# Storing the third group's norm factors in place of its scaled rows, and loading the mixer output's input straight into its low parts

## The chip, the cores and the metric

The kernel runs on one core of a Trainium2 chip. The metric is device time in microseconds for one execution of the whole program, the median of three runs; smaller is better. The core has a matrix engine (PE, with weight loads, PEld, beside it), VectorE (DVE), ScalarE (ACT), GpSimd (POOL) and a queue that issues the transfers (SP).

## What is computed

One inference step of a two-layer decoder, for a prompt of 1024 tokens with 16 learned tokens ahead of it and eight single-token sequences, 1048 columns in all, model width 1024. Layer 0 mixes tokens with a Conformer convolution, layer 1 with an RWKV-7 recurrence; each is followed by a squared-ReLU MLP. The parts that the change touches, from the reference:

```python
def _rmsnorm(x, g):
    xf = x.astype(jnp.float32)
    y = xf * lax.rsqrt(jnp.mean(xf * xf, axis=-1, keepdims=True) + RMS_EPS)
    return (y * g.astype(jnp.float32)).astype(x.dtype)
...
    xx = prev - h
    xr = h + xx * x_mix[0]
...
    out = ((yn + bonus).astype(h.dtype) * g) @ w_o
...
        hn = _rmsnorm(h, norm_mix[i])
...
        h = h + out
        h = h + _sqrelu_mlp(_rmsnorm(h, norm_mlp[i]), w_mlp_in[i], w_mlp_out[i])
```

In layer 1 the first argument of the mixer is the scaled row `_rmsnorm(h, norm_mix[1])`, and the residual that its output is added to is the unscaled `h`.

## The kernel before

Activations lie as 128 partitions (features) by 8 blocks (k) by tokens. Each matrix product is made of three matmuls of float32 rounded to a shorter type: every operand x is split into a high part (a cast on ACT, L159 and L177) and a low part (x minus the high part, L160 for activations and L182 for weights, on DVE or, in four pieces of 256 columns, on POOL), and `mm3` (L209 to L213) adds high·high, high·low and low·high.

The work comes in token groups. Layer 0 has three (columns 0 to 351, 352 to 699, 700 to 1047), the RWKV mixer four (0, 272, 528 and 784 onwards, 272, 256, 256 and 264 wide), mixer output and second MLP three (16, 344, 696 onwards, 328, 352, 352 wide). The mixer groups don't end where layer 0's do: mixer group 2 (528 to 783) begins in layer 0's second group and ends in its third.

At the end of layer 0 `norm_out` (L636 to L654) stores a group's MLP output to DRAM twice: unscaled to d_h (L640) and, after sums of squares on ACT, a mean on PE and a reciprocal on DVE (rs_d, L295), scaled in place by eight DVE instructions (L651, one per k) to d_hn (L654). For the third group this runs beside mixer group 0. `prepare` (L854 to L893) then loads a mixer group's scaled rows from d_hn as one tile hx (L863, L865), forms xx, the difference to the token before (L869), and later the mixes (mx, L892). For groups 1 to 3 it runs beside the v products of the group before.

Beside the mixer groups runs the recurrence over chunks of 64 tokens: loads of a chunk's factors (L1273 to L1284), a triangular inversion for every eight chunks (ni loaded at L1241, 30 pairs of DVE instructions tt and ni at L1246 and L1247, then stored to d_p at L1250 and loaded by chunk as p at L1280 and transposed to x on DVE at L1302), and per chunk a sequence of small matmuls (S, Y, gg, bT, W, po, U). `norm_gate` (L1507 to L1541) turns 128 tokens of its output into the mixer output's input and stores that to d_z.

`mixer_out` (L1629 to L1647) then, for each of the three output groups, loads h1 from d_h (L1633), loads d_z in eight pieces into temporary tiles zr of which there are three (L1639), splits each into z_h and z_l, and makes eight output columns (ps_oo) from the weights wo_0 to wo_7, adding each into h1 (L1643). The last chunks and the second MLP's first weights run beside the first of these groups. The pools used here are opened over memory that the mixer's input pools (hx, mixes and others) gave back, so that a tile can wait for the last user of the memory beneath it.

In each engine's queue instructions stand in the order that a scheduler gives them from the program's order, so a small edit can move others.

Of the kernel before, what the change touches and what calls it, by code (L numbers as in the profile page):

```python
# [16 lines left out]
P = 128  # L17
# [31 lines left out]
def hybrid_step(tc, x_prompt, x_sample, state_conv, state_shift, state_wkv, meta_tokens,  # L49
# [10 lines left out]
    with ctx:  # L60
# [12 lines left out]
        dram = pool(ctx, "dram", 1, space=bass.MemoryType.DRAM)  # L73
        d_x2 = dram.tile([P, KT, G0[2][1]], F32, name="d_x2")
        d_h = dram.tile([P, KT, T], F32, name="d_h")
        d_hn = dram.tile([P, KT, T], F32, name="d_hn")
        d_rk = dram.tile([P, KT, 2, T], F32, name="d_rk")
        d_ab = dram.tile([NCH, P, KT, 2, 2 * HS], F32, name="d_ab")
        d_v = dram.tile([NCH * HS, D], F32, name="d_v")
# [68 lines left out]
        def raw_pool(stack, tag, n, **kw):  # L148
            return pool(stack, f"wraw{tag}", 1, **kw), n

        def split_pool(stack, tag, n, **kw):
            return pool(stack, f"wsp{tag}", 1, **kw), n
# [74 lines left out]
        def dense(w, act, n, name, fill=None):  # L227
            it = dense_steps(w, act, n, name)
            while True:
# [4 lines left out]
                if fill:  # L234
                    fill()

        def new_act(pl, name, nmax, tag="act"):
            return (pl.tile([P, KT, nmax], F32R, name=f"{name}_h", tag=f"{tag}h"),
                    pl.tile([P, KT, nmax], F32R, name=f"{name}_l", tag=f"{tag}l"))

# [173 lines left out]
        with ExitStack() as le:  # L414
# [221 lines left out]
            def norm_out(g):  # L636

                c0, n = G0[g]
                hv = h[g][:, :, :n]
                nc.sync.dma_start(d_h[:, :, c0:c0 + n], hv)  # L640
                if g < 2:
                    add, parts = square_sums(n, f"d{g}", lambda k: u[g][:, k, :n], (nc.gpsimd,), "accd")
                else:
                    add, parts = square_sums(n, f"d{g}", lambda k: tt(f"sqd{k}", "t1")[:, :n], (nc.gpsimd, nc.vector))
                for k in range(KT):
                    add(k, hv[:, k, :])
                    yield MW / KT
                rs = rstd_of(mean_bcast(parts, n, f"d{g}"), n, 0, f"d{g}", "rs" if g < 2 else "rsm")
                yield 1
                for k in range(KT):  # L650
                    nc.vector.scalar_tensor_tensor(hv[:, k, :], hv[:, k, :], vec("norm_mix", KT + k), rs[:, :n],  # L651
                                                   op0=ALU.mult, op1=ALU.mult)
                    yield 1
                nc.sync.dma_start(d_hn[:, :, c0:c0 + n], hv)  # L654
# [199 lines left out]
        def prepare(g):  # L854

            c0, n = G1[g]
            npr = min(c0 + n, NP_TOK) - c0
            nm = lambda s, *a: f"{s}{g}" + "".join(f"_{x}" for x in a)

            hx = hnp.tile([P, KT, 1 + N1], F32, name=nm("hx"), tag="hx")  # L860
            if g == 0:
                nc.gpsimd.memset(hx[:, :, 0:1], 0.0)
                nc.sync.dma_start(hx[:, :, 1:1 + n], d_hn[:, :, :n])  # L863
            else:
                nc.sync.dma_start(hx[:, :, :1 + n], d_hn[:, :, c0 - 1:c0 + n])  # L865
            yield
            xx = hnp.tile([P, KT, N1], F32, name=nm("xx"), tag="xx")
            for k in range(KT):
                (nc.gpsimd if k % 3 == 2 else nc.vector).tensor_sub(xx[:, k, :npr], hx[:, k, 0:npr], hx[:, k, 1:1 + npr])  # L869
                yield  # L870
            if npr < n:
                sst = cur["raw"].tile([P, D], F32, name="sst", tag="raw")
                nc.scalar.dma_start(sst[:DEC, :], state_shift[0])
                pv = bank("pv", "x")
                for k in range(KT):
                    nc.tensor.transpose(pv[:, k * DEC:(k + 1) * DEC], sst[:DEC, k * P:(k + 1) * P], ident[:DEC, :DEC])
                sps = hnp.tile([P, KT, DEC], F32, name=nm("sps"), tag="sps")
                nc.scalar.copy(sps.rearrange("p k b -> p (k b)"), pv[:, :KT * DEC])
                nc.vector.tensor_sub(xx[:, :, npr:n], sps, hx[:, :, 1 + npr:1 + n])
                so = cur["raw"].tile([P, D], F32, name="so", tag="raw")  # L880
                for half in range(2):
                    pv = bank(f"pso{half}", "x")
                    for q in range(4):
                        nc.tensor.transpose(pv[:DEC + 1, q * P:(q + 1) * P], hx[:, half * 4 + q, npr:npr + DEC + 1], ident)
                    nc.scalar.copy(so[:DEC + 1, half * 512:(half + 1) * 512], pv[:DEC + 1, :])
                nc.scalar.dma_start(o_shift_prompt[0], so[0:1, :])
                nc.scalar.dma_start(o_shift_sample[0], so[1:DEC + 1, :])

            def mix(i, k):

                t = (cur["mx"] or cur["tmp"]).tile([P, cur["wm"]], F32, name=nm("mx", i, k), tag="t2")
                nc.vector.scalar_tensor_tensor(t[:, :n], xx[:, k, :n], vec("x_mix", i * KT + k), hx[:, k, 1:1 + n],  # L892
                                               op0=ALU.mult, op1=ALU.add)  # L893
                hi, lo = (r.tile([P, cur["wm"]], F32R, name=nm("m" + q, i, k), tag="m" + q) for q, r in zip("hl", cur["mix"]))
                split(hi[:, :n], lo[:, :n], t[:, :n], nc.gpsimd if k % 3 else nc.vector)
                return hi[:, :n], lo[:, :n]

            prep[g] = mix, hx, sps if npr < n else None
# [714 lines left out]


        with ExitStack() as l1:
            raw_f, wsp_f = raw_pool(l1, "f", 3), split_pool(l1, "f", 1)
            open_tmp(l1, N2, "2", 3)
            residp = pool(l1, "resid1", 1)
            actp = pool(l1, "actp1", 1)
            hidp = pool(l1, "hidp1", 2)  # L1620
            lf = l1.enter_context(ExitStack())
            wsp_g = split_pool(lf, "g", 1)
            cur.update(rings((raw_a, raw_f), (wsp_a, wsp_f, wsp_g)))
# [5 lines left out]
            def mixer_out(g, residp, actp, fill, add, order=range(KT), early=None):  # L1629
                ready = None  # L1630
                lo, n = G2[g]
                h1 = hl[g] = residp.tile([P, KT, cur["wide"]], F32, name=f"h1_{g}", tag="h")
                nc.sync.dma_start(h1[:, :, :n], d_h[:, :, lo:lo + n])  # L1633
                if early:
                    ready = early(h1)
                z = new_act(actp, f"z{g}", cur["wide"])
                for p in range(KT):
                    t = tt(f"zr{g}{p}", "t1")
                    nc.sync.dma_start(t[:, :n], d_z[:, p, lo:lo + n])  # L1639
                    split(z[0][:, p, :n], z[1][:, p, :n], t[:, :n], nc.vector)  # L1640
                for i, m in enumerate(order):
                    ps = dense(load_col(rwkv_w_o[0], m, f"wo{g}_{m}", nc.vector if early else nc.gpsimd), z, n, f"oo{g}_{m}", fill)
                    nc.vector.tensor_add(h1[:, m, :n], h1[:, m, :n], ps[:, :n])  # L1643
                    add(i, h1[:, m, :n])
                    if ready:
                        ready(m)
                    fill()  # L1647
# [326 lines left out]
```

## Time and profile before

| | |
|---|---|
| median of 3 runs | 2756.64 us (2746.97 to 2761.95) |
| the profiled execution | 2760.69 us |
| its span in the trace | 2758.7 us |
| granted PE clock, mean over the span | 0.971 |
| PE busy | 2585.6 us (94%) |
| PEld busy | 2495.6 us (90%) |
| DVE busy | 2074.5 us (75%) |
| POOL busy | 1710.2 us (62%) |
| ACT busy | 1404.5 us (51%) |
| mean DRAM traffic | 155 GB/s |

All times in the trace are microseconds from the span's start. PE, busy 94% of the span, is the engine whose gaps the profile is read for: a gap names the engine that released it, and a low granted clock behind a gap makes the matmuls there longer. A row of a timeline is one instruction or several equal ones, with its start, its time, engine, line, operation, result and operands; what stands in brackets is the idle time ahead of it and who ended that.

### The profile page before, as it was taken

Reading aid. Unit: us, or ns where it says so; the run is one execution under the profiler, and the core shown is the slowest. Engines: PE = TensorE matmul, PEld = TensorE weight load, DVE = VectorE, ACT = ScalarE, POOL = GpSimd, SP = SyncE. Lnnn points to the kernel's source line nnn. Section 1 sums busy time; section 2 is a strip of 40 time slices with the busy share of each in tenths; the row PEclk is TensorE's granted clock in tenths of the full one; section 3 lists DMA queues with packets and bytes.
Section 4 is the critical chain, followed back from the end, with each engine's and each line's share of the span. In section 5 each row is a group of like instructions: output and inputs, shape, how many; then the busy total and the mean of one; then the engine's idle time right before and its main releaser. Section 6 shows DMA issues by size and latency. Waiting matters only on the chain.

```text
span 2758.7 us, 54194 instructions
## 1 busy us (share of the span) xinstructions
PE 2585.6 (94%) x20362; PEld 2495.6 (90%) x20362; DVE 2074.5 (75%) x3868; ACT 1404.5 (51%) x2614; POOL 1710.2 (62%) x2259
## 2 busy tenths in 40 slices
PE   8998999999998999997898798979989999999998
PEld 7998999899997999996788687768989998999998
DVE  5999999997456554677988887677897687566565
ACT  5545444553355444565675775655544564333333
POOL 6686877887787444554553544547648856556663
PEclk9998999999999999999999999989999999999999
DMA  6563544445445446668796886887657642222221
GB/s 181 159 192 92 161 132 137 134 148 164 138 131 150 146 142 179 185 199 220 204 241 187 219 221 175 198 230 186 178 140 232 175 131 78 76 70 77 69 77 58
DMA packets 659283, 428.30 MB, mean 155 GB/s; under 512 B 126840, under 2 KB 609208, under 8 KB 659022
## 3 DMA queue, kind: packets, MB, share of 16 engines
q1 hardware_dynamic: 652780, 421.93, 55.0%
q10 hardware_dynamic: 6018, 2.89, 0.4%
q8 instruction: 160, 2.62, 0.4%
q14 instruction: 101, 0.83, 0.1%
q0 software_dynamic: 224, 0.03, 0.0%
HBM read 353.03 MB, written 72.66 MB: 154 GB/s over the span
## 4 chain that ended last, share of the span: by engine, by line
PE 64%; DVE 15%; DMA 7%; POOL 5%; ACT 4%; issue 4%; SPq 0%; POOLq 0%; ACTq 0%; DVEq 0%
PE ps_in L212 4%; PE ps_in L213 4%; PE ps_in L211 4%; PE out L212 4%; PE out L213 4%; PE out L211 4%; PE os L213 3%; PE os L211 3%; PE os L212 3%; POOL wo_lo L182 2%; POOL wi_lo L182 2%; DVE cv L552 2%; PE su L211 1%; PE su L213 1%; PE su L212 1%
## 5 line engine op out<-in xcount | busy, mean ns | idle before, releaser
L182 POOL TENSOR_TENSOR wo_lo<-wo_raw,wo_hi 128x256 fp32r<-128x256 f32 x512 | 398.1, 810 | 188.1 <-ACT wo_hi L177 149.0
L182 POOL TENSOR_TENSOR wi_lo<-wi_raw,wi_hi 128x256 fp32r<-128x256 f32 x472 | 373.3, 824 | 161.0 <-ACT wi_hi L177 150.3
L552 DVE SCALAR_TENSOR_TENSOR cv<-u,wdw,cv 128x352 f32<-128x352 f32 (+2 forms) x720 | 376.4, 572 | 0.7
L211 PE MATMUL out<-hh,wo_hi 128*128 128x348 f32 (+2 forms) x1024 | 332.2, 328 | 17.8 <-DVE h L382 6.9
L212 PE MATMUL out<-hh,wo_lo 128*128 128x348 f32 (+2 forms) x1024 | 330.8, 324 | 2.6 <-DVE wo_lo L182 2.6
L211 PE MATMUL ps_in<-m_h,wi_hi 128*128 128x348 f32 (+2 forms) x1024 | 329.7, 322 | 2.2 <-ACT wi_hi L177 1.4
L212 PE MATMUL ps_in<-m_h,wi_lo 128*128 128x348 f32 (+2 forms) x1024 | 328.6, 321 | 2.4 <-POOL wi_lo L182 2.4
L213 PE MATMUL ps_in<-m_l,wi_hi 128*128 128x348 f32 (+2 forms) x1024 | 327.8, 321 | 0.0
L213 PE MATMUL out<-hl,wo_hi 128*128 128x348 f32 (+2 forms) x1024 | 327.1, 323 | 0.0
L382 DVE TENSOR_TENSOR h<-h,out 128x348 f32<-128x348 f32 (+2 forms) x512 | 249.8, 503 | 68.8 <-PE out L213 68.1
L177 ACT CAST wo_hi<-wo_raw 128x1024 fp32r<-128x1024 f32 x152 | 159.3, 1049 | 203.0 <-PE ps_in L213 104.9
L177 ACT CAST wi_hi<-wi_raw 128x1024 fp32r<-128x1024 f32 x128 | 134.2, 1049 | 235.0 <-PE out L213 105.2
L211 PEld LDWEIGHTS out<-hh,wo_hi 128*128 128x128 f32 x1024 | 194.0, 190 | 24.7 <-DVE h L382 8.2
L212 PEld LDWEIGHTS out<-hh,wo_lo 128*128 128x128 f32 x1024 | 195.1, 191 | 4.5 <-DVE wo_lo L182 3.2
L211 PEld LDWEIGHTS ps_in<-m_h,wi_hi 128*128 128x128 f32 x1024 | 192.8, 188 | 4.6 <-ACT wi_hi L177 2.6
L212 PEld LDWEIGHTS ps_in<-m_h,wi_lo 128*128 128x128 f32 x1024 | 192.6, 188 | 3.8 <-POOL wi_lo L182 2.8
L213 PEld LDWEIGHTS out<-hl,wo_hi 128*128 128x128 f32 x1024 | 193.5, 190 | 1.0 <-DVE hl L160 0.5
L213 PEld LDWEIGHTS ps_in<-m_l,wi_hi 128*128 128x128 f32 x1024 | 192.3, 188 | 0.8 <-DVE m_l L305 0.2
L1859 DVE TENSOR_TENSOR h<-h,os 128x352 f32<-128x352 f32 x256 | 126.5, 515 | 58.7 <-PE os L213 58.2
L212 PE MATMUL os<-hhs,wos_lo 128*128 128x352 f32 x512 | 165.1, 323 | 0.0
L213 PE MATMUL os<-hls,wos_hi 128*128 128x352 f32 x512 | 164.1, 323 | 0.0
L211 PE MATMUL os<-hhs,wos_hi 128*128 128x352 f32 x512 | 155.3, 323 | 0.1
(501 smaller groups left out, 8040.3 us busy)
## 6 DMA issues: line engine op xcount, KB each, us to landing
wi_raw<-in_w_mlp_in_dram SPq DMA_DIRECT2D x128, 512.0 KB
wo_raw<-in_w_mlp_out_dram SPq DMA_DIRECT2D x128, 512.0 KB
wk_raw<-in_rwkv_w_k_dram SPq DMA_DIRECT2D x32, 512.0 KB
wr_raw<-in_rwkv_w_r_dram SPq DMA_DIRECT2D x32, 512.0 KB
wv_raw<-in_rwkv_w_v_dram SPq DMA_DIRECT2D x32, 512.0 KB
d_ab<-ab SPq DMA_DIRECT2D x32, 512.0 KB
ws_raw<-in_w_mlp_in_dram SPq DMA_DIRECT2D x32, 512.0 KB
wos_raw<-in_w_mlp_out_dram SPq DMA_DIRECT2D x32, 512.0 KB
```

What stands on the lines that cost most here:

```text
L177: nc.scalar.copy(hi[:, :a * b], raw[:, :a * b])
L182: eng_lo.tensor_sub(lo[:, cs], raw[:, cs], hi[:, cs].bitcast(F32))
L211: nc.tensor.matmul(ps, w[0], act[0], start=first, stop=False, **kw)
L212: nc.tensor.matmul(ps, w[1], act[0], start=False, stop=False, **kw)
L213: nc.tensor.matmul(ps, w[0], act[1], start=False, stop=last, **kw)
L382: nc.vector.tensor_add(hv[:, 4 * i + m, :], hv[:, 4 * i + m, :], ps[:, :n])
L552: nc.vector.scalar_tensor_tensor(acc[m][:, :n], ug[:, m, j:j + n], wdw[:, m, j:j + 1], acc[m][:, :n], op0=ALU.mult, op1=ALU.add)
L1859: nc.vector.tensor_add(hv[:, 4 * i + m, :], hv[:, 4 * i + m, :], ps[:, :n])
```

## The change

It has four parts.

1. The third group of `norm_out` stores its rms factors rs_d (128 by 348) to a new DRAM tensor d_rs and ends; the eight scalings and the store of the scaled rows are gone for that group, and d_hn holds 700 columns.
2. `prepare` loads group 0's rows in two halves (k 0 to 3 and 4 to 7). For groups 2 and 3 the columns from 700 on come unscaled from d_h, with their factors from d_rs, and are scaled in place by eight DVE instructions: 84 columns of group 2 (its other 173 come scaled from d_hn) and all 265 of group 3.
3. In `mixer_out` each piece of d_z is loaded into the low part's own tile and split in place, without a temporary tile; h1's load is issued after the second piece. High and low parts are 16 tiles (one per k) instead of two.
4. The pools of the mixer output are opened in another order: the activations' pool (z, and m of the second MLP) first, the weights' pools last.

```diff
-        d_hn = dram.tile([P, KT, T], F32, name="d_hn")
+        d_hn = dram.tile([P, KT, G0[2][0]], F32, name="d_hn")
+        d_rs = dram.tile([P, G0[2][1]], F32, name="d_rs")
...
         def new_act(pl, name, nmax, tag="act"):
+            if pl in in_parts:
+                tiles = [[pl.tile([P, nmax], F32R, name=f"{name}_{q}{k}", tag=f"{tag}{q}{k}") for q in "hl"] for k in range(KT)]
+                return tuple(Parts(list(t)) for t in zip(*tiles))
...
                 rs = rstd_of(mean_bcast(parts, n, f"d{g}"), n, 0, f"d{g}", "rs" if g < 2 else "rsm")
                 yield 1
+                if g == 2:
+                    nc.sync.dma_start(d_rs, rs[:, :n])
+                    return
                 for k in range(KT):
...
-                nc.sync.dma_start(hx[:, :, 1:1 + n], d_hn[:, :, :n])
+                for k in range(0, KT, 4):
+                    nc.sync.dma_start(hx[:, k:k + 4, 1:1 + n], d_hn[:, k:k + 4, :n])
             else:
-                nc.sync.dma_start(hx[:, :, :1 + n], d_hn[:, :, c0 - 1:c0 + n])
+                a, e, b = c0 - 1, c0 + n, G0[2][0]
+                if a < b:
+                    nc.sync.dma_start(hx[:, :, :min(b, e) - a], d_hn[:, :, a:min(b, e)])
+                if e > b:
+                    b = max(a, b)
+                    w, o = e - b, b - a
+                    rs = cur["tmp"].tile([P, N1], F32, name=nm("rsx"), tag="t2")
+                    nc.sync.dma_start(rs[:, :w], d_rs[:, b - G0[2][0]:e - G0[2][0]])
+                    nc.sync.dma_start(hx[:, :, o:o + w], d_h[:, :, b:e])
+                    for k in range(KT):
+                        hk = hx[:, k, o:o + w]
+                        nc.vector.scalar_tensor_tensor(hk, hk, vec("norm_mix", KT + k), rs[:, :w], op0=ALU.mult, op1=ALU.mult)
+                        if k % 4 == 3:
+                            yield
...
+            actp = pool(l1, "actp1", 1)
+            in_parts.append(actp)
+            open_tmp(l1, N2, "2", 3)
+            hidp = pool(l1, "hidp1", 2)
+            residp = pool(l1, "resid1", 1)
             raw_f, wsp_f = raw_pool(l1, "f", 3), split_pool(l1, "f", 1)
-            open_tmp(l1, N2, "2", 3)
-            residp = pool(l1, "resid1", 1)
-            actp = pool(l1, "actp1", 1)
-            hidp = pool(l1, "hidp1", 2)
...
-                nc.sync.dma_start(h1[:, :, :n], d_h[:, :, lo:lo + n])
...
                 for p in range(KT):
-                    t = tt(f"zr{g}{p}", "t1")
-                    nc.sync.dma_start(t[:, :n], d_z[:, p, lo:lo + n])
-                    split(z[0][:, p, :n], z[1][:, p, :n], t[:, :n], nc.vector)
+                    zh, zl = z[0][:, p, :n], z[1][:, p, :n]
+                    nc.sync.dma_start(zl.bitcast(F32), d_z[:, p, lo:lo + n])
+                    split(zh, zl, zl.bitcast(F32), nc.vector)
+                    if p == 1:
+                        nc.sync.dma_start(h1[:, :, :n], d_h[:, :, lo:lo + n])
```

The change also moves instructions in the queues. Line numbers behind the change are higher by 1 up to L237 and by 17 to 37 below it.

On DVE, beside mixer group 0, where rs_d is made (ml and mx are mixes of group 1, wk_2_lo a weight's low part, rk and ab factors of the recurrence). Before:

```order
L295 RECIPROCAL rs_d_14249<-sd_d_14247 128x348
L160 TENSOR_TENSOR ml_2_6_14405<-mx_2_6_14402,mh_2_6_14404 128x256
L1126 TENSOR_TENSOR n_6_14284<-nn_6_14286,nmask 128x128
L1135 TENSOR_TENSOR n_6_14284<-nm_6_14304,nmask 16x16 x2
L1142 TENSOR_TENSOR bv_6_14313<-vv_6_14139,pk_6_14311 128x272
L1172 SCALAR_TENSOR_TENSOR rk_7_14050<-rk_7_14050,negs,pb_7_14315 128x272
L651 SCALAR_TENSOR_TENSOR h_2_9452<-h_2_9452,pvec,rs_d_14249 128x348 x8
L182 TENSOR_TENSOR wk_2_lo<-wk_2_raw,wk_2_hi 128x1024
L892 SCALAR_TENSOR_TENSOR mx_0_0_14963<-xx_12911,pvec,hx_12876 128x256
```

The same place with the change:

```order
L313 RECIPROCAL rs_d_14251<-sd_d_14249 128x348
L161 TENSOR_TENSOR ml_2_6_14399<-mx_2_6_14396,mh_2_6_14398 128x256
L1161 TENSOR_TENSOR n_6_14283<-nn_6_14285,nmask 128x128
L1170 TENSOR_TENSOR n_6_14283<-nm_6_14303,nmask 16x16 x2
L1177 TENSOR_TENSOR bv_6_14312<-vv_6_14141,pk_6_14310 128x272
L1207 SCALAR_TENSOR_TENSOR rk_7_14052<-rk_7_14052,negs,pb_7_14314 128x272
L927 SCALAR_TENSOR_TENSOR mx_0_0_14957<-xx_12913,pvec,hx_12878 128x256
L183 TENSOR_TENSOR wk_2_lo<-wk_2_raw,wk_2_hi 128x1024
```

The row of eight scalings is gone; what stood behind it follows at once.

On PE, where the mixer output begins (pk belongs to the last mixer group's factors; yn, S, Y, gg, bT, W and po to the recurrence and its output norm). Before:

```order
L1140 MATMUL pk_7_22539<-rk_7_22501,hsum 128x264
L1533 MATMUL yn_0_22854<-ident,ey_0_22711 128x128
L1365 MATMUL S_22889<-uv,bkt_22284 64x64 x16
L1365 MATMUL Y_22890<-sv,xa_14461 64x64 x16
L1365 MATMUL Y_22890<-uv,nr_21381 64x64 x16
L1317 MATMUL gg_22891<-x_22835,no_22306 32x32 x16
L1533 MATMUL yn_0_22854<-ident,ey_0_22711 128x128 x3
L1357 MATMUL bT_23038<-ident,bk_22301 128x128 x4
L1357 MATMUL bT_23044<-ident,bk_22301 128x128 x4
L1365 MATMUL W_23138<-sv,xa_14464 64x64 x16
L1317 MATMUL po_23139<-p_22307,gg_22892 32x32 x16
L211 MATMUL ps_oo_0_22639<-z_h,wo_0_hi 128x328
```

With the change, where sixteen of the mixer output's matmuls stand between pk_7 and yn (their last four are shown):

```order
L213 MATMUL ps_oo_1_22761<-z_h_22612,wo_1_lo 128x328
L214 MATMUL ps_oo_1_22761<-z_l_22613,wo_1_hi 128x328
L212 MATMUL ps_oo_1_22761<-z_h_22614,wo_1_hi 128x328
L213 MATMUL ps_oo_1_22761<-z_h_22614,wo_1_lo 128x328
L1568 MATMUL yn_0_22875<-ident,ey_0_22732 128x128
L1400 MATMUL S_22910<-uv,bkt_22299 64x64 x16
L1400 MATMUL Y_22911<-sv,xa_14455 64x64 x16
L1400 MATMUL Y_22911<-uv,nr_21396 64x64 x16
L1352 MATMUL gg_22912<-x_22856,no_22321 32x32 x16
L214 MATMUL ps_oo_0_22660<-z_l_22615,wo_0_hi 128x328
L212 MATMUL ps_oo_0_22660<-z_h_22616,wo_0_hi 128x328
L213 MATMUL ps_oo_0_22660<-z_h_22616,wo_0_lo 128x328
```

The mixer output's first matmuls move ahead of that run of the recurrence, between whose pieces the rest of them now stand.

On DVE at the inversion beside the mixer output (tt and ni are its pairs, counted down to tt_1; m_l is the second MLP's input). Before, at the inversion's end:

```order
L1246 TENSOR_TENSOR tt_1_24172<-ni_22652 128x30
L1247 TENSOR_TENSOR ni_22652<-ni_22652,tt_1_24172 128x30
L1643 TENSOR_TENSOR h_0_22594<-h_0_22594,ps_oo_5_23074 128x328
L288 TENSOR_TENSOR acc_m_22982<-acc_m_22982,sq_5_23104 128x328
L1643 TENSOR_TENSOR h_0_22594<-h_0_22594,ps_oo_6_23122 128x328
L1643 TENSOR_TENSOR h_0_22594<-h_0_22594,ps_oo_7_23232 128x328
L305 SCALAR_TENSOR_TENSOR m_l<-h_0_22594,pvec,m_h 128x328 x7
```

With the change, around the inversion's twentieth pair:

```order
L1680 TENSOR_TENSOR h_0_22609<-h_0_22609,ps_oo_6_23143 128x328
L1282 TENSOR_TENSOR ni_22673<-ni_22673,tt_12_24055 128x12x19
L1281 TENSOR_TENSOR tt_11_24079<-ni_22673 128x220
L323 SCALAR_TENSOR_TENSOR m_l_23318<-h_0_22609,pvec,m_h_23317 128x328
L1282 TENSOR_TENSOR ni_22673<-ni_22673,tt_11_24079 128x11x20
L323 SCALAR_TENSOR_TENSOR m_l_23320<-h_0_22609,pvec,m_h_23319 128x328
L1281 TENSOR_TENSOR tt_10_24099<-ni_22673 128x210
L323 SCALAR_TENSOR_TENSOR m_l_23322<-h_0_22609,pvec,m_h_23321 128x328
```

The last additions and m_l stood behind all 30 pairs and now stand among them. On SP the eight loads of z move ahead of five weights of the mixer output, of the inversion's load of ni, and of h1's load.

## Rows read from the trace of the kernel before

**Rows 1.** The page: the chain of work that ended last, by engine.

```profile
PE 64%; DVE 15%; DMA 7%; POOL 5%; ACT 4%; issue 4%; SPq 0%; POOLq 0%; ACTq 0%; DVEq 0%
```

**Rows 2.** Windows: length, busy time by engine (instructions), granted clock, DMA share, GB/s.

```profile
1245.00:1275.00 30.00, 17.37 (x175) 15.40 (x175) 25.95 (x45) 17.87 (x45) 20.55 (x29) 0.83 0.79 206
1255.00:1265.00 10.00, 2.11 (x39) 1.38 (x40) 10.00 (x17) 2.11 (x6) 7.09 (x9) 0.67 0.76 227
```

**Rows 3.** DVE timeline around the third group's scalings.

```profile
1250.87 5.92 DVE L651 SCALAR_TENSOR_TENSOR h<-h,pvec,rs_d 128x348 f32<-128x348 f32 x8
...
1257.84 1.26 DVE L892 SCALAR_TENSOR_TENSOR mx<-xx,pvec,hx 128x256 f32<-128x256 f32 x3
...
1263.29 0.78 DVE L1204 TENSOR_TENSOR ab<-wa,em 128x512 f32<-128x512 f32 x2
```

**Rows 4.** PE timeline at the same place.

```profile
1260.01 1.22 PE L1040 MATMUL pn<-sq,hsel 128*128 128x256 f32 x2 [6.71 <-ACT sq L1050]
1264.11 0.65 PE L1122 MATMUL nn<-ab 64*32 64x32 f32 x32 [2.88 <-DVE ab L1204]
```

**Rows 5.** DVE timeline at the first uses of hx, mixer groups 0 and 2.

```profile
883.48 1.41 DVE L869 TENSOR_TENSOR xx<-hx 128x272 f32<-128x272 f32 x2 [5.77 <-DMA hx<-d_hn]
...
1358.29 4.13 DVE L869 TENSOR_TENSOR xx<-hx 128x256 f32<-128x256 f32 x6 [0.68 <-DMA hx<-d_hn]
```

**Rows 6.** PE timeline behind group 0's hx.

```profile
892.57 0.81 PE L211 MATMUL out<-hh,wo_hi 128*128 128x348 f32 x3 [4.08 <-ACT wo_hi L177]
895.74 0.66 PE L212 MATMUL out<-hh,wo_lo 128*128 128x348 f32 x1 [2.36 <-DVE wo_lo L182]
```

**Rows 7.** Windows where groups 2 and 3 are prepared.

```profile
1345.00:1385.00 40.00, 31.24 (x299) 26.83 (x297) 33.07 (x62) 25.06 (x63) 23.10 (x30) 0.87 0.80 222
1540.00:1600.00 60.00, 49.22 (x676) 44.17 (x676) 54.38 (x108) 46.15 (x114) 19.90 (x30) 0.94 0.94 249
```

**Rows 8.** Chain in order of time: loads of hx (start, time, what).

```profile
874.85 8.61 DMA hx<-d_hn
...
1538.17 7.24 DMA hx<-d_hn
```

**Rows 9.** Windows at the mixer output of the first group.

```profile
1808.00:1885.00 77.00, 56.44 (x613) 51.38 (x613) 59.56 (x124) 34.41 (x70) 41.80 (x53) 0.82 0.79 212
1820.00:1842.00 22.00, 10.00 (x92) 9.11 (x93) 12.63 (x34) 6.84 (x16) 7.01 (x9) 0.54 1.07 275
1830.00:1850.00 20.00, 13.36 (x69) 12.88 (x70) 17.36 (x50) 5.80 (x16) 0.00 (x0) 0.70 0.90 252
1860.00:1880.00 20.00, 17.99 (x181) 17.57 (x181) 19.53 (x31) 8.64 (x16) 19.85 (x24) 0.91 0.76 183
```

**Rows 10.** PE timeline: the mixer output's first matmul.

```profile
1836.64 0.64 PE L211 MATMUL ps_oo<-z_h,wo_hi 128*128 128x328 f32 x1 [10.74 <-ACT z_h L159]
```

**Rows 11.** Groups on DVE, 1830 to 1850 and 1860 to 1882 (busy, mean ns).

```profile
L1246 DVE TENSOR_TENSOR tt<-ni 128x238 f32<-128x238 f32 (+13 forms) x16 | 5.5, 345 | 0.4
...
L1246 DVE TENSOR_TENSOR tt<-ni 128x210 f32<-128x210 f32 (+9 forms) x10 | 6.5, 648 | 0.2
```

**Rows 12.** DVE timeline: one size of tt early and late, the inversion's end, chunk 13.

```profile
1830.95 0.25 DVE L1246 TENSOR_TENSOR tt<-ni 128x84 f32<-128x84 f32 x1
...
1876.76 0.99 DVE L1246 TENSOR_TENSOR tt<-ni 128x84 f32<-128x84 f32 x1
...
1881.28 0.65 DVE L1247 TENSOR_TENSOR ni<-ni,tt 128x30 f32<-128x30 f32 x1
...
1885.12 4.84 DVE L305 SCALAR_TENSOR_TENSOR m_l<-h,pvec,m_h 128x328 fp32r<-128x328 f32 x7 [0.93 <-ACT m_h L304]
...
1904.91 0.45 DVE L1302 STREAM_TRANSPOSE x<-p 128x256 f32<-128x256 f32 x1 [0.15 <-PE po L1317]
```

**Rows 13.** SP timeline: the inverse stored and loaded by chunk.

```profile
1881.99 0.34 SPq L1250 DMA_DIRECT2D d_p<-ni  x1
1884.63 0.37 SPq L1280 DMA_DIRECT2D p<-d_p  x1
```

More of the change, by code (lines that the diff above doesn't have):

```diff
@@ L235, in dense, with __init__, __getitem__ @@
                     fill()
+        class Parts:
+            def __init__(self, tiles):
+                self.tiles = tiles
+            def __getitem__(self, at):
+                rows, k, cols = at
+                if isinstance(k, slice):
+                    return Parts([t[rows, cols] for t in self.tiles[k]])
+                return self.tiles[k][rows, cols]
+        in_parts = []
         def new_act(pl, name, nmax, tag="act"):
+            if pl in in_parts:
+                tiles = [[pl.tile([P, nmax], F32R, name=f"{name}_{q}{k}", tag=f"{tag}{q}{k}") for q in "hl"] for k in range(KT)]
+                return tuple(Parts(list(t)) for t in zip(*tiles))
             return (pl.tile([P, KT, nmax], F32R, name=f"{name}_h", tag=f"{tag}h"),
```

## The prediction
> **What bounds the kernel now.** I read the page first: PE is busy 94% of the span and carries 64% of the chain that ended last, DVE 15%, transfers 7% [rows 1]. So the kernel is PE's matmuls and a few dozen gaps, and an edit is worth what it takes out of a gap, or out of the low clock behind one. I then looked for the gaps at the places that the change touches, in windows, and for who ends each in the timelines of PE and DVE. There are three such places, and at each the reader should see which engine is full while PE is not. At 1255 to 1265 us PE is busy 2.11 of 10 us, DVE 10.00 [rows 2]. Behind group 0's hx PE waits 4.08 and 2.36 us [rows 6]. In the 77 us where the mixer output begins PE is busy 56.44 us at a clock of 0.82, and in the 22 us from 1820 on 10.00 us at 0.54 [rows 9].
>
> **The third group's factors in place of its rows.** Removed are eight scalings, 5.92 us of DVE in one block [rows 3], and a store of 1.43 MB (128 x 8 x 348 x 4 bytes). Behind the block, in DVE's order, come a weight's low part, the mixes and the factors ab. PE waits 6.71 us for a square that follows from those mixes, and 2.88 us for ab [rows 4]. Since DVE has no free time there, all that follows comes 5.9 us earlier, and the longer wait shrinks to below 1 us. Over the 30 us around it PE is busy 17.37 us at a mean clock of 0.83 [rows 2]; at full clock the same work would take 17.37 x 0.83 = 14.4 us, so up to 3.0 us lies in the clock. I take 0.6 of it, because the 2.88 us wait behind it stays. Gain **6.5 us**; the ends are 3 (half the block is replaced by the next wait, 2.88) and 8.9 (5.9 and the whole clock). The store's time is counted at nothing: the waits of rows 4 name ACT and DVE, no transfer; if that cover is gone it is worth up to 2.
>
> **Scaling what is loaded.** In return groups 2 and 3 scale in place: 8 instructions on 84 columns and 8 on 265. No row has these shapes. The mix, the same operation on 256 columns, takes 1.26 / 3 = 0.42 us [rows 3], so the eight of group 3 take 3.4 us; by the removed block's 5.92 / 8 = 0.74 they would take 5.9. For 84 columns the nearest row is tt at 0.25 us, at worst 0.99 [rows 12]: 2.0 us, at worst 7.9. I take 3.4 and 2.0, the prices of the same operation and of the smaller size undisturbed. How much reaches PE goes by how full DVE is there: 33.07 of 40 us around group 2, 54.38 of 60 around group 3 [rows 7], so 0.83 x 2.0 + 0.91 x 3.4 = 4.8. The new order puts the recurrence's masks and some factors ahead of group 3's scalings, so I take **-4 us**. Ends: 0 (both lie in DVE's free time) and -10 (4.8 at the dear prices, 0.83 x 7.9 + 0.91 x 5.9 = 11.9, less the idle time in which some of it falls). The transfers are two more for group 2 and one more for group 3, of which the factors' is small; xx of group 2 now waits for two loads where it waited 0.68 us for one [rows 5], and the loads take 5.61 to 8.61 us where the chain shows them (two of three are among the rows) [rows 8]. That is inside the bad end. What stands behind these scalings on DVE is xx and with it the next group's mixes.
>
> **Group 0 in two halves.** The load takes 8.61 us [rows 8], DVE waits 5.77 us for it [rows 5], and behind xx stand the splits hl and the products r of the running MLP, for which PE in turn waits [rows 6]. The first half may land some 4 us earlier; then DVE's three xx of the first four k (the fourth is POOL's), 3 x 0.7 = 2.1 us by 1.41 / 2 [rows 5], go into the wait, and what stands behind comes up to 2.1 us earlier. But the second half lands when the whole one did, and PE's longer wait names a weight's cast on ACT. I take **+1 us**, ends -1 (one more issue on SP in front of everything there) and +3.
>
> **The mixer output.** PE's first matmul there waits 10.74 us for z_h [rows 10], because the loads of z stood behind six weights' loads, the inversion's ni and h1, in three temporary tiles. Now they come first, and PE has 16 matmuls of two columns to do before the recurrence's next step. PE alone could gain up to the 77 - 56.4 = 20.6 us of idle time [rows 9] and a few more from the clock; since the weights wo_2 to wo_4 now stand behind eight loads, I put PE's own limit at 15.
>
> What is late next is DVE's inversion. The added m_l and the last additions now stand among its pairs: eight m_l at 4.84 / 7 = 0.69 [rows 12] and three additions at about 0.5 are 7.0 us, less the eight z_l, some 4 us, that leave it: +3 us. And its first half ran while POOL was idle, 0.00 of 20 us [rows 9]; there a tt took 345 ns in the mean, and 648 ns in 1860 to 1882 [rows 11], where POOL was busy 19.85 of 20 [rows 9]. At one size it is 0.25 against 0.99 [rows 12]. With the products earlier, POOL's splits of wo_5 to wo_7 come earlier too and fall on that first half: 33 instructions by 0.30 is 10 us, of which I take half. So the inversion's end moves from 1881.9 to about 1890. From there the store, p's issue at 1884.63 (2.7 us later) [rows 13] and a landing of some 5.6 us (the shortest load in rows 8, an estimate that is rather long for p) make 8.3 us to chunk 13's transposition: 1898. Before, that ran at 1904.91 and waited 0.15 us for PE, not for p [rows 12]. So DVE lets PE come forward by at most 1904.9 - 1898 = 7 us. I take **+6 us**, ends 0 and 15. For the second and third output groups I count nothing, as their loads were already covered by PE's work.
>
> **Sum.** 6.5 - 4 + 1 + 6 = 9.5 us against the profiled execution's 2760.7, so 2751.2. That execution was 4 us above the median of the runs; against the median the forecast is 2756.6 - 9.5, about **2747 us**.
>
> **The rivals.**
>
> *The inversion doesn't bind* (2734). If POOL doesn't slow the first half, or chunk 13 has more slack, the mixer output gives 15; with 8 for the block, 2 for the halves and -2 for the scalings that is 23 us. For it speaks that the end of the inversion had some 15 us of slack (1904.9 less 1884.6 and a landing) [rows 12, 13]. Against it, that DVE is busy 17.36 of 20 us in the first half already [rows 9].
>
> *POOL binds DVE* (2753). If every one of those 33 instructions takes the dear price, the inversion ends at 1895, p is there at 1903, and the mixer output gives 2 at most, I take 0: 6.5 - 4 + 1 = 3.5 us. The row for it is the same tt at 0.25 us with POOL idle and 0.99 with POOL busy [rows 9, 12]. The Trainium skill, page "SBUF — State Buffer", section "Who interferes with whom", says that a VectorE instruction with two inputs in SBUF contends with a GpSimd instruction that reads SBUF, and that whichever starts first holds the shared ports for its whole instruction. By that rule bringing POOL's splits onto the pairs gives back what the earlier z gains; this trace agrees with it so far as those two rows go.
>
> *The inversion is late, and the recurrence with it* (2765, slower). On SP ni's load now stands behind eight loads of 168 kB, at 212 GB/s [rows 9] some 6 us. Then the inversion ends at 1881.9 + 3 + 10 + 6 = 1901, x is there at 1909, and PE stands at chunk 13 for longer than before: -4.4; with the scalings at -10 and the block at 6.5 it is 8 us slower. It decides from an end of the inversion later than 1904.9 - 8.3 = 1896.6. Against it, DVE had idle time before the inversion that the z splits fill.
>
> *z doesn't come early* (2751). The last pieces' tiles lie over memory that the mixer's small products used, so their loads wait for PE; if that holds the products up, the mixer output gives 2 and the sum is 5.5.
>
> **How the numbers follow.** Chances: forecast 0.38, the inversion not binding 0.27, POOL binding DVE 0.17, the late inversion 0.12, z not early 0.06. A measurement of this kernel tells a difference from about 0.5%, 13.8 us: below 2742.8 or above 2770.4. A quarter of the forecast's case (0.10) and nearly all of the second lie below: 0.37 faster. Above lie half of the late inversion (0.06) and some of the other cases with the scalings at their bad end (0.03): 0.09. The rest, 0.54, is no change that can be told. The range reaches from a little below the second case, 2731, to the late inversion, 2766; the bounds of the single terms, all on one side, would give 2728 and 2765.
>
> **What would show it.** Right: no block of eight scalings near 1250 and no wait over 2 us ahead of pn; ps_oo's first matmul within 2 us of pk's last; tt of the first pairs longer than 0.3 us beside a busy POOL; the inversion's end between 1885 and 1895 on the old clock, that is, less what was gained ahead of it; hx's scalings of groups 2 and 3 as two groups of eight with about 0.25 and 0.42 us each. Wrong: chunk 13's transposition waiting several us for p, or PE's first matmul still waiting for z_h; DVE waiting for the factors' load in group 2 or 3; the longer wait ahead of pn replaced by one of the same size.

## The result, and the profile after

| | before | with the change |
|---|---|---|
| median (6 runs each, side by side) | 2755.21 us | 2783.39 us (2775.1 to 2793.08) |
| ratio, 95% interval | 1 | 1.0102 [1.0075, 1.0128] |
| the profiled execution | 2760.69 us | 2779.47 us |
| its span | 2758.7 us | 2777.7 us |

The change costs 28 us, where 9.5 less was forecast, and the time lies outside the range. The two traces are single executions, 19 us apart. Lines of the page with the change: the span, the busy time of each engine, and the chain by engine:

```profile
span 2777.7 us, 54208 instructions
...
PE 2603.5 (94%) x20362; PEld 2505.9 (90%) x20362; DVE 2070.2 (75%) x3876; ACT 1403.0 (51%) x2614; POOL 1710.1 (62%) x2259
...
PE 24%; DVE 6%; POOL 4%; DMA 3%; issue 2%; ACT 2%; SPq 0%; POOLq 0%; ACTq 0%; DVEq 0%
```

PE has 18 us more of busy time (2585.6 before), and the span grew by 19: PE hardly waits more than before. That is the first thing to see, since a late load or a late engine would have shown as waiting. The chain of waits [rows 1] adds up to 41% of this span, where it covered nearly all of it before, so I looked for the place with marks that both traces have, the stores of the inverse (d_p) and the transpositions x of two chunks:

| mark | before | with the change | difference |
|---|---|---|---|
| d_p, first | 1288.47 | 1284.94 | -3.5 |
| d_p, second | 1346.40 | 1345.00 | -1.4 |
| d_p, third | 1497.88 | 1515.40 | +17.5 |
| d_p, fourth | 1701.33 | 1710.31 | +9.0 |
| chunk 11's x (ahead of the mixer output) | 1781.53 | 1801.07 | +19.5 |
| d_p, fifth (beside the mixer output) | 1881.99 | 1913.61 | +31.6 |
| chunk 13's x | 1904.91 | 1925.28 | +20.4 |
| span | 2758.7 | 2777.7 | +19.0 |

The loss arises between the second and the third store, beside mixer group 1's v product, where the diff touches nothing. Part of it is made up at the fourth store, and ahead of the mixer output it stands at 19.5 again. Differences of a few us say little in such a table: the reciprocal that makes rs_d, ahead of everything that part 1 edits, starts at 1247.04 before, at 1244.01 with the change, and at 1243.09 in a later kernel that has parts 3 and 4 alone.

The windows beside the v product, with the columns of [rows 2], before:

```profile
1400.00:1430.00 30.00, 26.90 (x413) 23.70 (x400) 27.65 (x52) 24.03 (x62) 12.07 (x16) 1.00 0.91 248
```

With the change:

```profile
1400.00:1430.00 30.00, 30.00 (x267) 21.84 (x262) 12.32 (x21) 14.40 (x32) 3.40 (x5) 0.77 0.58 140
1401.40:1412.00 10.60, 10.60 (x89) 7.29 (x84) 4.95 (x8) 5.18 (x13) 2.11 (x2) 1.00 0.90 231
1416.00:1421.60 5.60, 5.60 (x27) 3.47 (x26) 0.00 (x0) 0.16 (x1) 0.00 (x0) 0.50 0.08 19
```

PE is busy for the whole 30 us and does 267 matmuls where 413 were done in 26.90. DVE falls from 27.65 to 12.32 us, ACT from 24.03 to 14.40, POOL from 12.07 to 3.40, and the transfers from 248 to 140 GB/s. PE's timeline with the change shows what it does there:

```profile
1405.84 0.38 PE L212 MATMUL p_v<-mh,wv_hi 128*128 128x256 f32 x1
1406.16 0.33 PE L1400 MATMUL Y<-uv,nr 128*64 128x64 f32 x2
1406.41 0.39 PE L213 MATMUL p_v<-mh,wv_lo 128*128 128x256 f32 x1
1406.74 0.33 PE L1400 MATMUL Y<-uv,nr 128*64 128x64 f32 x2
...
1411.75 0.38 PE L213 MATMUL p_v<-mh,wv_lo 128*128 128x256 f32 x1
1412.06 0.24 PE L1352 MATMUL gg<-x,no 32*32 32x32 f32 x2
1412.23 0.39 PE L214 MATMUL p_v<-ml,wv_hi 128*128 128x256 f32 x1
...
1416.29 0.58 PE L214 MATMUL p_v<-ml,wv_hi 128*128 128x256 f32 x1
1416.81 0.32 PE L1352 MATMUL gg<-x,no 32*32 32x32 f32 x4
1417.05 0.58 PE L212 MATMUL p_v<-mh,wv_hi 128*128 128x256 f32 x1
```

Before, the same matmuls stand in runs:

```profile
1396.55 0.28 PE L211 MATMUL p_v<-mh,wv_hi 128*128 128x256 f32 x1
1396.67 0.28 PE L212 MATMUL p_v<-mh,wv_lo 128*128 128x256 f32 x1
...
1418.24 1.15 PE L1365 MATMUL Y<-sv,xa 128*64 128x64 f32 x32
1419.23 1.10 PE L1365 MATMUL Y<-uv,nr 128*64 128x64 f32 x32
1420.26 0.69 PE L1317 MATMUL gg<-x,no 32*32 32x32 f32 x32
```

A p_v starts 0.12 us after the one before it, and 32 matmuls of Y take about 1 us, so a p_v and two of Y take 0.18 us in runs. Alternating, the next p_v starts 0.57 us later (1405.84 to 1406.41). With gg as the neighbour it is 0.48 us at the full clock (1411.75 to 1412.23), and 0.76 us once the clock has fallen to 0.50 of full speed, which is 1.2 GHz (1416.29 to 1417.05). From 1401.4 to 1421.6 PE spends 20.2 us on work that takes about 6.4 us in runs, an estimate from these spacings. That is 14 us too many, for 61 changes between large matmuls and small ones in this stretch of the trace. They come from the scheduler's order of PE, which the prediction read at the edited places alone. With the change:

```
L212 MATMUL p_v_16340<-mh_3_0_15658,wv_6_hi 128x256
L1400 MATMUL Y_17069<-uv,nr_16661 64x64
L213 MATMUL p_v_16340<-mh_3_0_15658,wv_6_lo 128x256
L1400 MATMUL Y_17069<-uv,nr_16661 64x64
```

The Trainium skill, page "TensorEngine Tiling (Array Packing)", section "Key Properties", says that changing the tiling mode drains TensorE. The step from 0.18 to 0.57 us per round is in line with it; a drain as such does not show in the trace, which has all of the time as busy.

DVE, which the next part of the recurrence needs, has nothing to do meanwhile:

```profile
1405.50 1.40 DVE L1452 TENSOR_TENSOR sv<-fs,sw 64x512 f32<-64x512 f32 x2 [0.46 <-PE Y L1400]
1422.70 0.29 DVE L1161 TENSOR_TENSOR n<-nn,nmask 128x128 f32<-128x128 f32 x1 [15.79 <-PE nn L1157]
```

PE's nn, which ends the 15.79 us, stands behind the alternation in PE's queue.

### The profile page after: what moved, and what is told of

It is laid out like the page before. It is cut to its first block, busy times and chain, and to the rows that moved or that the text cites. A ratio compares the mean times of both kernels' runs of the same rounds, so it can differ in the third digit from the quotient of the medians.

```text
span 2777.7 us, 54208 instructions
## 1 busy us (share of the span) xinstructions
PE 2603.5 (94%) x20362; PEld 2505.9 (90%) x20362; DVE 2070.2 (75%) x3876; ACT 1403.0 (51%) x2614; POOL 1710.1 (62%) x2259
```

## The experiments

Three theories stood at the start: (1) the loss is the alternation on PE; (2) it is the mixer output with its late inversion; (3) it is the third group's factors and their scalings. Ratios are to the kernel before, run beside them on the same chip (in the order of the sets, its medians were 2760.69, 2762.22 and 2759.89 us in the three sets of runs).

**One load for group 0.** The change, with the halves of part 2 undone:

```diff
-                for k in range(0, KT, 4):
-                    nc.sync.dma_start(hx[:, k:k + 4, 1:1 + n], d_hn[:, k:k + 4, :n])
+                nc.sync.dma_start(hx[:, :, 1:1 + n], d_hn[:, :, :n])
```

> The changed kernel with one edit undone: group 0's rows are loaded in one transfer again. In the order of this version PE's matmuls for the v product of mixer group 1 no longer alternate one by one with the recurrence's small Y and gg matmuls (90 changes between the two kinds in that stretch with the change, about 24 here). Theory 1, the alternation costs the time: the 21 us lost between 1408 and 1498 in the trace come back, the clock stays near 1 there, and the time is 2755 to 2765. Theory 2, the late inversion at the mixer output costs it, and whatever is lost earlier is made up: no change, 2775 to 2790. Theory 3, the scalings of groups 2 and 3 cost it: no change either, 2775 to 2790.

Measured: 2761.42 us, 1.0003 [0.9991, 1.0014]. With one load in place of two, 500 us ahead of the place, the order has no such alternation, and the time is level with before. The window is nearly as before again:

```profile
1400.00:1430.00 30.00, 25.54 (x449) 22.94 (x448) 26.87 (x46) 22.53 (x58) 11.18 (x18) 0.97 0.92 227
```

**The old mixer output.** Parts 3 and 4 undone; of the edit the splits are shown:

```diff
-                    nc.sync.dma_start(zl.bitcast(F32), d_z[:, p, lo:lo + n])
-                    split(zh, zl, zl.bitcast(F32), nc.vector)
+                    t = tt(f"zr{g}{p}", "t1")
+                    nc.sync.dma_start(t[:, :n], d_z[:, p, lo:lo + n])
+                    split(z[0][:, p, :n], z[1][:, p, :n], t[:, :n], nc.vector)
```

> The changed kernel with the mixer output's input and pools as before (16 tiles, loads into the low parts and pool order undone). The alternation on PE stays in its order. Theory 1: the stretch from 1408 to 1498 stays long, and 2770 to 2785 is measured. Theory 2: the late inversion is gone, and with it the loss: 2750 to 2760. Theory 3: 2775 to 2790.

Measured: 2779.68 us, 1.0071 [1.0059, 1.0083]; PE is busy 30.00 of the 30 us. The alternation and most of the loss stay: theory 2 falls as the main cause. Whether the new mixer output adds something beside the alternation can't be told, as the intervals of 1.0071 and of the change's 1.0102 overlap.

**Parts alone.** First the halves in the kernel before:

```diff
-                nc.sync.dma_start(hx[:, :, 1:1 + n], d_hn[:, :, :n])
+                for k in range(0, KT, 4):
+                    nc.sync.dma_start(hx[:, k:k + 4, 1:1 + n], d_hn[:, k:k + 4, :n])
```

> The kernel before with group 0's load in two halves and nothing else. The alternation is not in its order. Theory 1: within 5 us of before, 2750 to 2760, so that it is not the halves themselves that cost the time. If the halves cost it by another way than PE's order: 2775 or more. Theories 2 and 3: no change, 2750 to 2760.

Measured: 2761.55 us, 0.9999 [0.9990, 1.0009]. The halves alone do nothing that can be measured. Then parts 3 and 4 alone, the edit of the second experiment turned round (its added lines):

```diff
+                    nc.sync.dma_start(zl.bitcast(F32), d_z[:, p, lo:lo + n])
+                    split(zh, zl, zl.bitcast(F32), nc.vector)
```

> The kernel before with the mixer output's edits alone (16 tiles, loads into the low parts, pools reordered). The alternation is not in its order. Theory 1: what is gained up to the second MLP's sums, some 18 us, is given back at the wait for the inverse behind it: 2750 to 2762. Theory 2: the late inversion costs more than the loads give, 2770 to 2785. My forecast's case: 6 us faster, 2745 to 2752.

Measured: 2756.47 us, 0.9985 [0.9975, 0.9994], 4 us faster and by its ratio the fastest complete version of the study. Last the third group's factors, without the halves and the mixer output (of the edit the store is shown):

```diff
+                if g == 2:
+                    nc.sync.dma_start(d_rs, rs[:, :n])
+                    return
```

> The kernel before with the first part and the loads of groups 2 and 3 alone (factors stored in place of rows, columns from 700 on scaled by whoever loads them); one load for group 0, mixer output as before. No long alternation in its order. By my terms, 6.5 for the block less 4 for the scalings: 2.5 us faster. By the first batch (everything but the halves is level with before, the mixer output alone 4 us faster), these parts cost about 5 us: 2758 to 2768. Theory 3, the scalings cost the 20 us: 2775 or more.

Measured: 2761.20 us, 0.9996 [0.9988, 1.0005]. Theory 3 falls as well: the factors with their scalings come out level, and the cost of 5 us that I had expected lies outside the interval.

**No scalings.** The last kernel without its sixteen scalings of loaded rows:

```diff
-                    for k in range(KT):
-                        hk = hx[:, k, o:o + w]
-                        nc.vector.scalar_tensor_tensor(hk, hk, vec("norm_mix", KT + k), rs[:, :w], op0=ALU.mult, op1=ALU.mult)
-                        if k % 4 == 3:
-                            yield
+                    yield
+                    yield
```

> As e6_factors_alone without the sixteen scalings of groups 2 and 3: their columns from 700 on are used unscaled, so that part of the result is left out of the computation; the loads stay. If the removed block of eight scalings is worth 6.5 us and nothing takes its place: 2747 to 2753. If the block was covered, level with before, and then the difference to e6 is what the sixteen scalings cost, 4 by my term.

Measured: 2750.75 us, 0.9958 [0.9945, 0.9971]. Without the block, the store and the new scalings the kernel is 11.6 us faster than before, and the scalings cost about 10.5 of them (2761.20 less 2750.75), with whatever their instructions move in the queues.

**Another number for all bursts.** `burst` gives the recurrence's matmuls a priority ahead of the rest. With a larger number they might stand in one piece everywhere. In the change, and in the kernel before, the same edit:

```diff
-        BURST = 400
+        BURST = 1000
```

> The changed kernel, whole, with one number edited: BURST, the priority with which the recurrence's groups of small matmuls are put ahead in the order, from 400 to 1000. All data, loads and operations are those of the change; in PE's order the stretch with 90 changes between large and small matmuls has some 20. Theory 1, the alternation alone costs the 20 us: 2750 to 2765. Theory 1b, it is the halves together with the new loads of groups 2 and 3 in some other way (a transfer, a wait on DVE) and the alternation only goes along with it: 2775 to 2790.

> The kernel before with BURST at 1000 and nothing else: 232 changes between large and small matmuls in PE's order in place of 252, 13 in place of 26 in its longest such stretch. Theory 1 at some 0.25 us for each change that is gone (20 us for about 80 in the changed kernel): 5 us faster, 2750 to 2757. If the number of changes doesn't matter: level, or other by what the new order moves.

Measured: 2790.85 us, 1.0100 [1.0083, 1.0117] for the change, and 2780.05 us, 1.0059 [1.0046, 1.0072] for the kernel before, where I had expected a gain. Both expectations were missed. The number has a price of its own, so the pair settles little about the alternation. But neither kernel has it, and the change is still 10.8 us slower than the kernel before beside it: in these orders the change costs something that the alternation does not explain, and no run says what. In the second kernel's timeline of PE the bursts now stand ahead of other work and wait for their factors, 19.6 us in all for bk in place of 7.5 before:

```profile
1421.15 2.81 PE L1290 MATMUL A<-xa,bk 128*128 128x256 f32 x6 [3.77 <-DMA bk<-d_ab]
...
1533.50 1.19 PE L1290 MATMUL A<-xa,bk 128*128 128x256 f32 x2 [6.99 <-DMA bk<-d_ab]
```

So the number was changed for one burst alone, in three kernels that share this edit:

```diff
-        def burst(lead, rest):
+        def burst(lead, rest, ahead=BURST):
-            with tc.high_priority(offset=BURST):
+            with tc.high_priority(offset=ahead):
```

**The alternation taken out.** The change, with chunk 1's burst in one piece:

```diff
-            burst(ss[:2], rest)
+            burst(ss[:2], rest, 1000 if c == 1 else BURST)
```

> The changed kernel, whole, with the priority of one single burst raised from 400 to 1000: the group of S, Y and gg matmuls of the recurrence's chunk 1, the one that alternates with the v product. PE's order then has 248 changes between large and small matmuls in place of 322. Theory 1, at 20 us for the alternation (some 0.28 us for a change): 21 us less than the changed kernel, ratio to before 1.000 to 1.004. Theory 1b, the cause is another joint effect of the halves and the new loads: ratio 1.008 to 1.012.

Measured: 2765.90 us, 1.0021 [1.0009, 1.0033]. Against the change's 1.0102 that is 0.8%, 22 us, from one burst's place in PE's queue, with every part of the change kept.

**The alternation put in.** The first experiment's kernel, with chunk 1's burst at 325:

```diff
-            burst(ss[:2], rest)
+            burst(ss[:2], rest, 325 if c == 1 else BURST)
```

> The version of e1_one_load (level with before) with the priority of that one burst lowered from 400 to 325, and nothing else: 296 changes between large and small matmuls in place of 236. Theory 1 at 0.28 us each: 17 us slower than e1_one_load, ratio to before 1.005 to 1.008. Theory 1b: level, 0.999 to 1.002.

Measured: 2773.02 us, 1.0046 [1.0032, 1.0061], 12 us more than without it, in the expected direction and just below the expected range. The window of this kernel, and below it that of the kernel with the alternation taken out:

```profile
1400.00:1430.00 30.00, 30.00 (x294) 21.57 (x294) 18.88 (x32) 17.45 (x41) 6.03 (x11) 0.87 0.65 162
```

```profile
1400.00:1430.00 30.00, 27.12 (x432) 23.32 (x431) 22.85 (x42) 22.12 (x56) 9.99 (x18) 0.94 0.97 236
```

**The alternation put into the kernel before.** There the burst's neighbour is the k product:

```diff
-            burst(ss[:2], rest)
+            burst(ss[:2], rest, 250 if c == 1 else BURST)
```

> The kernel before with the priority of that one burst lowered from 400 to 250, and nothing of the change: 286 changes between large and small matmuls in place of 252, 36 of them in one stretch where the burst's Y and gg matmuls alternate with a k product. Theory 1 at 0.28 us each: 10 us slower, ratio 1.002 to 1.005. Theory 1b: level, 0.999 to 1.002.

Measured: 2760.74 us, 1.0000 [0.9989, 1.0011]; the expectation was missed. Its window beside the same one of the kernel before, which stands second:

```profile
1415.00:1431.00 16.00, 16.00 (x189) 11.58 (x185) 15.74 (x26) 9.86 (x26) 11.75 (x14) 0.84 0.91 226
```

```profile
1415.00:1431.00 16.00, 13.50 (x257) 11.50 (x257) 15.91 (x27) 13.85 (x35) 12.77 (x14) 1.00 0.95 248
```

PE does 189 matmuls in place of 257 and its clock falls, but DVE stays as busy as it was, 15.74 against 15.91 us. DVE, nearly full in both, had work that did not stand behind the alternation. In the change DVE is busy 12.32 of 30 us at the corresponding place. Hence a narrower theory, made after this miss: the alternation costs the kernel what it starves, not what PE spends on it. It fits these runs, but none was made to test it. The stretch here is also shorter, 35 changes in the trace against 61 in the change and 64 in the run before this one.

**Four loads.** The change, with group 0's rows in quarters:

```diff
-                for k in range(0, KT, 4):
-                    nc.sync.dma_start(hx[:, k:k + 4, 1:1 + n], d_hn[:, k:k + 4, :n])
+                for k in range(0, KT, 2):
+                    nc.sync.dma_start(hx[:, k:k + 2, 1:1 + n], d_hn[:, k:k + 2, :n])
```

> The changed kernel with group 0's rows loaded in four transfers in place of two. The order that comes out has 250 changes in place of 322 and no long alternation. Theory 1: as e1_one_load, ratio 0.998 to 1.003. Theory 1b, the load in parts together with the new loads costs the time: ratio 1.008 or more.

Measured: 2763.36 us, 1.0014 [1.0006, 1.0022]. With the rest of the change, one and four loads give an order without the alternation, and two give one with it. Four loads and one differ by about 3 us by their ratios, so the number of loads has no price here that explains the loss.

The third store of the inverse, in the traces: 1497.88 us before, 1515.40 with the change, 1493.99 with one load, 1496.56 with the alternation taken out, 1501.52 with four loads, 1519.68 with the old mixer output, 1507.08 with the alternation put in, and 1500.16 in the kernel before with it put in. The mark is latest where the alternation stands beside the v product, and in the kernel before it hardly moves. It is no measure of the alternation alone: with the larger number for all bursts it comes at 1512.13 and 1506.89, without an alternation.

## Why the prediction was wrong

**The step that failed.** The prediction went through the three places of the diff and took the queues everywhere else as unchanged. No term and no rival had PE's order beside mixer group 1. Of the 28 us, about 22 go when that alternation is taken out, with an uncertainty of some 8 us by the two intervals; put in, it cost 12. Without it the change stands at +1 to +6 us (1.0003 with one load, 1.0014 with four, 1.0021 with the one burst moved): level or a little slower, where a gain of 9.5 was forecast. The parts measured alone, 4 us faster, 1 us faster and level, don't add up to that, and the difference stays open. What is left is in the terms:

**The block of eight scalings (forecast +6.5).** The block is gone and PE's two waits shrink, as forecast. PE's timeline after, for [rows 4]:

```profile
1253.20 0.70 PE L1075 MATMUL pn<-sq,hsel 128*128 128x256 f32 x2 [2.21 <-ACT sq L1085]
...
1255.87 0.58 PE L1157 MATMUL nn<-ab 64*32 64x32 f32 x32 [1.97 <-DVE ab L1239]
...
1284.16 0.58 PE L212 MATMUL p_wa<-hxh,wa_hi 128*128 128x256 f32 x1 [3.23 <-ACT wa_hi L178]
```

The two waits are 4.18 us in place of 9.59; the longer one is 2.21, not below 1. Then a wait of 3.23 us at 1284 follows, where the kernel before waits 1.31 us at most from 1265 to 1290. What the block was worth at its place must be counted from what stands ahead of it on DVE, since that is early already. Before, and with the change:

```profile
1247.04 2.30 DVE L295 RECIPROCAL rs_d<-sd_d 128x348 f32<-128x348 f32 x1
```

```profile
1244.01 2.30 DVE L313 RECIPROCAL rs_d<-sd_d 128x348 f32<-128x348 f32 x1
```

The change is 3.0 us ahead there, 6.8 us ahead at pn and 3.5 us ahead at the first store. So PE gained 3.8 us at pn, where 5.9 were forecast, and at the first store 0.5 us is left of it. In the run without scalings nothing is left: 3.9 us ahead at the reciprocal (1243.19), 3.7 at the first store (1284.74). The term took a shorter wait for a gain of the kernel; by the first store the rest of the queues had taken it back. The 11.6 us of that run come later; its trace is 11.2 us ahead at the fourth store (1690.09 against 1701.33). Whether they are the store that no longer competes or another order of the queues was not separated.

**Scaling what is loaded (forecast -4).** The operation on 84 and on 265 columns, with the change:

```profile
1369.21 3.63 DVE L898 SCALAR_TENSOR_TENSOR hx<-hx,pvec,rsx 128x84 f32<-128x84 f32 x8
```

```profile
1561.52 5.64 DVE L898 SCALAR_TENSOR_TENSOR hx<-hx,pvec,rsx 128x265 f32<-128x265 f32 x8
```

That is 9.3 us in place of the 5.4 that I took: 0.45 and 0.71 us each, where I had taken 0.25 and 0.42. The mix's price [rows 3] was the wrong neighbour for group 3, and the removed block's 0.74 the right one; for group 2 the price of tt, another operation, was too low. The cost in time, 10.5 us, is at the term's bad end, and more than the 9.3 us themselves. That DVE is busy 83 and 91% of the time there [rows 7] fits this, but what the queues' order adds was not separated.

**The halves (forecast +1).** 0 from the halves alone, with an interval of some 2.7 us to either side, so that the forecast can't be told from nothing.

**The mixer output (forecast +6).** 4 us alone, and nothing beside the factors (1.0003 with both against 0.9996 without it). The first half of its mechanism came as forecast. PE's first matmul follows pk without a wait for z_h [rows 10]:

```profile
1831.33 0.85 PE L212 MATMUL ps_oo<-z_h,wo_hi 128*128 128x328 f32 x1
```

Then what is late next is the inversion, as the prediction named it. The inversion's first pair on DVE before, and the pairs as groups from 1820 to 1885:

```profile
1829.77 0.20 DVE L1246 TENSOR_TENSOR tt<-ni 128x30 f32<-128x30 f32 x1 [3.99 <-DMA ni<-d_n]
```

```profile
L1247 DVE TENSOR_TENSOR ni<-ni,tt 128x30 f32<-128x30 f32 (+14 forms) x30 | 14.7, 491 | 0.7
L1246 DVE TENSOR_TENSOR tt<-ni 128x30 f32<-128x30 f32 (+14 forms) x30 | 13.3, 445 | 4.6 <-DMA ni<-d_n 4.0
```

With the change (single instructions, and below them the pairs as groups from 1840 to 1914):

```profile
1851.28 0.67 DVE L1281 TENSOR_TENSOR tt<-ni 128x30 f32<-128x30 f32 x1 [11.15 <-DMA ni<-d_n]
...
1912.89 0.66 DVE L1282 TENSOR_TENSOR ni<-ni,tt 128x30 f32<-128x30 f32 x1
...
1925.28 0.45 DVE L1337 STREAM_TRANSPOSE x<-p 128x256 f32<-128x256 f32 x1 [2.94 <-DMA p<-d_p]
```

```profile
L1281 DVE TENSOR_TENSOR tt<-ni 128x30 f32<-128x30 f32 (+14 forms) x30 | 17.8, 593 | 11.7 <-DMA ni<-d_n 11.2
L1282 DVE TENSOR_TENSOR ni<-ni,tt 128x30 f32<-128x30 f32 (+14 forms) x30 | 16.4, 548 | 0.5
```

On the old clock (20 us less, by chunk 11's x) the inversion ends at 1893.5, inside the 1885 to 1895 that was named but 3.5 us behind the 1890 that was taken. It begins at 1831.3, 1.5 us later than before. DVE waits 11.15 us for ni in place of 3.99, but mostly since DVE is done earlier: ni's load is issued at 1841.91, on the old clock when it was before (1822.52), so the 6 us that the rival of the late inversion had for it did not come. The pairs take 34.2 us in place of 28.0, and the other work among them 3.9 us more. The way from the inversion's end to the transposition took 11.7 us, where 8.3 was forecast, and chunk 13 now waits for p. On SP six other issues now stand between the store and the load of p:

```profile
1913.61 0.34 SPq L1285 DMA_DIRECT2D d_p<-ni  x1
...
1919.23 1.28 SPq L1315 DMA_DIRECT2D p<-d_p  x1
```

5.6 us lie between the two where 2.6 did, with no issue between them [rows 13]. So the later end and the longer way use up the 7 us that the forecast had here: chunk 13 comes at 1905.3 on the old clock, when it came before, and the mixer output's gain is given back there. That chain is read from the traces; no run took it apart.

**POOL beside DVE.** The prediction's dear price held in kind: the first tt, 128x30, takes 0.67 us in place of 0.20, and the mean tt over the 30 pairs is 593 ns in place of 445. POOL, idle beside the first pairs before [rows 9], is busy 15.64 of the 20 us beside them now. PE is busy 11.62 of these 20, so its idle time of [rows 9] has in part moved here:

```profile
1851.00:1871.00 20.00, 11.62 (x115) 11.08 (x114) 19.00 (x33) 6.44 (x12) 15.64 (x21) 0.74 1.07 284
```

The pairs cost 6.2 us more in all, close to the 5 that were priced. That POOL is the reason is not shown by a run.

**The range.** It was built from the bounds of the named terms and the rivals. An edit that re-sorts the queues can change the order anywhere, by 20 us here, and the range had no width for that.

## What to carry to other kernels

Where a scheduler sets the order, compare the whole order of the bounding engine before and after, not only the edited places, and look on PE for large and small matmuls that change places one by one. In a profile such a stretch shows as an engine that is fully busy with fewer instructions per microsecond, and with the other engines falling idle beside it. In these runs it cost time where the other engines' work stood behind it, and none where DVE had other work. Before a change's parts are judged, the accident of the order is to be taken out of the comparison, here by moving one burst, since it was several times larger than what the complete parts are worth alone. And a wait that shrinks is not yet a gain: count from a mark ahead of the edit to one behind it.

## What was not expected of the hardware

- Matmuls of 128 x 128 (256 columns) that alternate with pairs of 64 x 64 (64 columns) take 0.57 us per round, against about 0.18 us for the same three in runs, at the full clock.
- All of that time counts as busy: 20.2 of 20.2 us. Yet the granted clock fell from 1.00 to 0.50 (2.4 to 1.2 GHz) during it, with PE never idle in the records. What PE did before it fell was 89 matmuls in 10.6 us, against 413 in 26.9 busy us before the change, where the clock stayed at 1.00.
- One load in two pieces has no measurable price in the kernel before (0.9999). In the change it came with some 20 us, by the scheduler's order and not by the load.
